# Early feed-forward work between expert matmuls: one piece for every second step, and the last pieces after the dynamic loop

## The chip, the core and the metric

The kernel runs on one NeuronCore of a Trainium2 chip. The metric is the device time of one execution, in microseconds (us). Three runs of the kernel before gave 2300.58, 2306.05 and 2307.99; the median is 2306.05. TensorE (PE) does the matmuls, ScalarE (ACT) and VectorE (DVE) the elementwise work and GpSimd (POOL) a little of it; SyncE (SP) issues the loads of the weights, in the order of its program.

## The reference, cut to what matters

The program computes two transformer blocks. The first ends in a mixture of 16 experts over 256 tokens, two experts for each token; the second begins with a half feed-forward layer on 256 latent tokens (the first block's output) and, with the same weights, on 256 context tokens (an input of their own):

```
# block 1, end: 16 experts, y added to h
for e in range(N_EXPERTS):
    hidden = jax.nn.silu(xt @ w_exp_gate[e]) * (xt @ w_exp_up[e])     # 1024 -> 512
    y = y + combine[:, e:e + 1] * (hidden @ w_exp_down[e])            # 512 -> 1024
# block 2, start: the same weights for latent (h_x) and context tokens (h_c)
h_x = _half_ffn(h_x, ..., ffn1_up[l], ffn1_down[l])
h_c = _half_ffn(h_c, ..., ffn1_up[l], ffn1_down[l])                   # D_FF = 2816
```

The context tokens don't depend on block 1. Their feed-forward work can therefore be done during the experts.

## The kernel before

**Early work.** The 2816 hidden channels are 22 tiles of 128, worked off in parts of 6, 6, 6 and 4 tiles. For the context tokens of the first layer the second part (6 tiles) is done early, by the generator `early_ffn` (L1036). It gives up control (`yield`) 32 times: 24 times in the up projection, each time after 12 matmuls of 256 columns (tile `pab`), and 8 times in the down projection, after 18 of them (`pd` from `eH`, `eL`). So there are 288 early up matmuls and 144 early down matmuls. The weights of a tile are first split in two by ACT (L225) and DVE or POOL (L228) into a tile `w`, of which there are two (`wspe`). `fill(n)` lets the generator run to its n-th next `yield`. Three calls with FILL = 3 stand ahead of the experts and use 9 of the 32.

**Experts.** `experts` (L1082) takes the 16 experts in 8 pairs (0 to 7). An expert works on up to 64 gathered tokens, so the two experts of a pair use one half of TensorE's columns each. In a pair:
- gate and up (tile `egu`, L1151): two halves of gate, two of up, called steps here; each step needs one chunk of 1 MB of each expert and has 8 rows in the built program (4 for each expert);
- silu on ACT (`es`, L1161), the product on DVE (L1162), a transpose on TensorE (`ept`, L1165), its copy on DVE (`hT`, L1168);
- down (tile `ey`, L1177): two steps with one chunk of each expert; the split of `y` by ACT and DVE; scatter to the tokens (`eo`, L1191 and L1192).

After pairs 0 and 2 stands the gather of the tokens of the next two pairs (`xgp`, 32 matmuls). `self.fill(1)` stands behind each of the six steps (L1155, L1180), so that 6 pieces are handed out in a pair, until there are no more.

**Loads.** `rawtile` gives a chunk one of seven 8 KB buffers, three in the pool `raw` and four in `rawm`, in a fixed alternation of the pools; two more tiles (`spare`) serve once. A buffer is free again when its last reader is done: a matmul for a chunk of an expert, the splits of both halves for a chunk of the early work. The early work's up weights are six chunks (three fetches of two), all fetched ahead of the experts; the third fetch lies in two of the four `rawm` buffers until it is split. The down weights are four chunks of 768 KB.

**The dynamic loop.** After pair 5 (LOOP_AT) a loop serves experts with more than 64 tokens (L1021 to L1027). In the profiled execution its body doesn't run. What stands behind it can't move ahead of it, and the seven chunks loaded ahead of it are the first of pair 6. The early work is used up there (L1017).

**What sets the order.** The program text gives priorities; a scheduler puts each engine's instructions in order by its own estimates when the program is built, and chooses the buffers. On the chip each engine follows its order.

Of the kernel before, what the change touches and what calls it, by code (L numbers as in the profile page):

```python
# [169 lines left out]
class Builder:  # L170
# [26 lines left out]
    def small(self, shape, name, dt=F32):  # L197
        return self.scr.tile(shape, dt, tag="sm_" + name, name=name, bufs=2)

    # ------------------------------------------------------------ weights  # L200
    def rawtile(self):
        if self.spare:
            return self.spare.pop(0)
# [72 lines left out]
                cons(c + i, p)  # L276
                yield True

    # ------------------------------------------------------------ norms
    def rsqrt(self, v, n, name):  # L280
        V = self.nc.vector
        y = self.small([128, n], name + "_y", I32)
# [99 lines left out]
        for _ in self.pending:  # L382
            pass

    # ------------------------------------------------------------ set-up
    def setup(self):
        nc, I = self.nc, self.I
        C = self.const
# [118 lines left out]
        o = self.voff[name] + j  # L507
        return self.vT[:, o:o + n]

    # ------------------------------------------------------------ modulation  # L510
    def ada(self, l, n, on_vector):
        V, mm = self.nc.vector, self.nc.tensor.matmul
        ps = self.mm("ada_ps")
# [58 lines left out]
        for l, n in lns:  # L572
            yield from self.ada(l, n, True)

    # ------------------------------------------------------------ feed-forward
    def ffn(self, l, n, up, dn, vs, side, pace, after):
        nc = self.nc
        self.raw_n, self.raws = 0, 7
# [105 lines left out]
        hs = self.h[:, d, v * S:(v + 1) * S]  # L684
        self.nc.vector.scalar_tensor_tensor(hs, p, self.gmod[:, l, n, d, v:v + 1], hs, ALU.mult, ALU.add)  # L685

    # ------------------------------------------------------------ block 1
    def to_tokens(self, src, dst, nt, ch0):
        nc = self.nc
        p = self.mm("tt")  # L690
        for t in range(nt):
            nc.tensor.transpose(p[:, t * 128:(t + 1) * 128], src[:, t * 128:(t + 1) * 128], self.ident)
        nc.scalar.activation(dst[:, 0:nt, ch0:ch0 + 128],
                             p[:, :128 * nt].rearrange("p (t c) -> p t c", c=128), AF.Copy)
# [267 lines left out]
        yield from self.proj(self.I["w_sb_out"][0], 0, 4, 0, 8, act, S,  # L962
                             lambda t, p: nc.vector.tensor_tensor(gates[:, t, :], p, gates[:, t, :], ALU.mult))

    # ------------------------------------------------------------ experts
    def moe(self):
        nc, I = self.nc, self.I
        V = nc.vector
        self.raw_n, self.raws = 0, 7
        with self.sub("hn", 1) as Q, self.sub("hide", PARTS[EARLY]) as E, self.sub("moe", 1) as P, \  # L970
                self.sub("wspe", 2) as self.wsp, self.sub("moew", 1) as W, self.sub("rawm", 4) as self.raw_more:
            hH = [Q.tile([128, 1024], F32R, name=f"hnH{t}") for t in range(2)]
            hL = [Q.tile([128, 1024], F32R, name=f"hnL{t}") for t in range(2)]
            rs = self.rs
            self.early = self.early_ffn(E)
            self.fill(FILL)
            comb, sel = self.route(self.lg, rs, P)
            self.fill(FILL)
            pp = self.mm("pos")
            nc.tensor.matmul(pp[:, 0:16], self.before, sel[:, 0, :], start=True, stop=True)  # L980
            nc.tensor.matmul(pp[:, 16:32], self.before, sel[:, 1, :], start=True, stop=False)
            nc.tensor.matmul(pp[:, 16:32], self.ones, sel[:, 0, :], start=False, stop=True)
            for t in range(2):
                nc.tensor.matmul(pp[:, 32:48], self.ones, sel[:, t, :], start=(t == 0), stop=(t == 1))
            mc = P.tile([128, 1], F32, name="mc")
            V.tensor_reduce(mc, pp[:, 32:48], AX.X, ALU.max)
            mi = P.tile([128, 1], I32, name="mi")
            V.tensor_scalar(mi, mc, -1.0, None, ALU.add)
            V.tensor_scalar(mi, mi, 6, None, ALU.logical_shift_right)
            pos = P.tile([128, 2, 16], F32, name="pos")  # L990
            V.scalar_tensor_tensor(pos, pp[:, :32].rearrange("p (t e) -> p t e", t=2), 1.0, sel,
                                   ALU.add, ALU.mult)
            V.tensor_scalar(pos, pos, -1.0, None, ALU.add)
            for t in range(2):
                for q in range(2):
                    p = self.a2("hnt")[:, 0, :] if q else self.mm("hnt")
                    for j in range(4):
                        nc.tensor.transpose(p[:, j * 128:(j + 1) * 128],
                                            self.h[:, q * 4 + j, t * 128:(t + 1) * 128], self.ident)
                    hi, lo = hH[t][:, q * 512:(q + 1) * 512], hL[t][:, q * 512:(q + 1) * 512]  # L1000
                    nc.scalar.activation(hi, p, AF.Copy, scale=rs[:, t:t + 1])
                    V.scalar_tensor_tensor(lo, p, rs[:, t:t + 1], hi.bitcast(F32), ALU.mult, ALU.subtract)
            self.fill(FILL)
            self.gates_of_route()
            order = [(p, c) for p in range(8) for c in range(12)]
            ready = {pc: self.expert_chunk(*pc) for pc in order[:AHEAD]}
            self.spare = [P.tile([128, 2048], F32, tag="xg", name="raw", bufs=2),
                          W.tile([128, 2048], F32, tag="y", name="raw")]
            ready.update({pc: self.expert_chunk(*pc) for pc in order[AHEAD:AHEAD + 2]})
            self.on_pool = 0  # L1010
            self.gs = P.tile([128, 8], F32, name="gs")
            pos2 = P.tile([128, 2, 16], F32, name="pos2")
            V.tensor_copy(pos2, pos)
            for p in self.experts(pos, comb, hH, hL, P, W, ready):
                if p != LOOP_AT:
                    continue
                for _ in self.early:  # L1017
                    pass
                ready.update({(p + 1, c): self.expert_chunk(p + 1, c) for c in range(7)})
                with self.tc.issue_after(self.loaded.ins):  # L1020
                    more = nc.values_load(mi[0:1, 0:1], min_val=0, max_val=3)  # L1021
                self.raw_loop = self.wsp
                with self.tc.If(more > 0):
                    with self.tc.For_i(0, more, 1):
                        V.tensor_scalar(pos2, pos2, -64.0, None, ALU.add)
                        for _ in self.experts(pos2, comb, hH, hL, P, W, {}):
                            pass  # L1027
                self.raw_loop = None
            self.raw_more = None
        self.pending = self.two_norms(self.sums)  # L1030

# [4 lines left out]
    def early_ffn(self, E):  # L1036
        nc, I = self.nc, self.I
        up, dn = I["ffn1_up_2"][0], I["ffn1_down_2"][0]
        f0, nf = sum(PARTS[:EARLY]), PARTS[EARLY]
        sl = slice(S, 2 * S)  # L1040
        hid = []

        def fetch(c):
            c0 = (f0 + 2 * c) * 128
            return [self.rows(up, 0, KD, m + c0, 256) for m in (0, NFF * 128)]

        nxt = fetch(0)
        for c in range(nf // 2):
            cur, nxt = nxt, fetch(c + 1) if 2 * c + 2 < nf else None
            for i in range(2):  # L1050
                p = self.mm("pab")
                for m in range(2):
                    w = self.split_w(cur[m][:, :, i * 128:(i + 1) * 128])
                    for ks in (range(4), range(4, KD)):
                        self.gemm(p[:, m * S:(m + 1) * S], w, self.xact(sl), ks=ks)
                        if m == 0 or ks[0] == 0:
                            yield True
                s, t = self.s512("fs")[:, :S], self.s512("ft")[:, :S]
                nc.scalar.activation(s, p[:, :S], AF.Silu)
                nc.vector.tensor_tensor(t, s, p[:, S:], ALU.mult)  # L1060
                hid.append([E.tile([128, S], F32R, tag=x, name=x) for x in ("eH", "eL")])
                self.split_a(*hid[-1], t)
                yield True
        for dc in range(4):
            v = self.rows(dn, f0 * 128, nf, dc * 256, 256)
            for i in range(2):
                w = self.split_w(v[:, :, i * 128:(i + 1) * 128])
                p = self.mm("pd")[:, :S]
                self.gemm(p, w, lambda f: hid[f])
                self.residual(p, 2 * dc + i, 0, 0, 1)  # L1070
                yield True

    def expert_chunk(self, p, c):
# [8 lines left out]
    def experts(self, pos, comb, hH, hL, P, W, ready):  # L1082
# [57 lines left out]
        for p in range(8):  # L1140
# [4 lines left out]
            for m in range(2):  # L1145
                for kh in range(2):
                    for aa in both:
                        w = {a: chunk(p, m * 4 + kh * 2 + a) for a in aa}
                        for kk in range(4):
                            for a in aa:  # L1150
                                mm(pr[a * 64:a * 64 + 64, m, :],  # L1151
                                   xg[p // 2][:, kh * 4 + kk, es[a] % 4 * 64:es[a] % 4 * 64 + 64], w[a][:, kk, :],
                                   start=(kh == 0 and kk == 0), stop=(kh == 1 and kk == 3))
                    if self.raw_loop is None:
                        self.fill(1)  # L1155
            if p % 2 == 0:
                slot_gates(p // 2)
# [12 lines left out]
            for fh in range(2):  # L1170
                for aa in both:
                    w = {a: chunk(p, 8 + fh * 2 + a) for a in aa}
                    for ff in range(2):
                        f = fh * 2 + ff
                        for n in range(2):
                            for a in aa:
                                mm(y[a * 64:a * 64 + 64, n, :], hT[:, f, a * 64:a * 64 + 64],  # L1177
                                   w[a][:, ff, n * 512:(n + 1) * 512], start=(f == 0), stop=(f == 3))
                if self.raw_loop is None:
                    self.fill(1)  # L1180
            y2 = W.tile([128, 2, 1024], F32R, tag="y", name="y")
            yH, yL = y2[:, 0, :], y2[:, 1, :]
# [123 lines left out]
        V.tensor_tensor(o1, o1, o2, ALU.add)  # L1306
        spread(comb, o1)

    # ------------------------------------------------------------ block 2 mixing
    def mix(self, l):  # L1310
        nc, I = self.nc, self.I
        full = l == 0
# [404 lines left out]
            nc.vector.tensor_scalar(z, p, self.vec("ps", l * 2 + j), None, ALU.mult)  # L1717
            self.split_a(self.xH[:, 2 + j, :NX], self.xL[:, 2 + j, :NX], z)

    # ------------------------------------------------------------ all of it  # L1720
    def finish(self):
        nc = self.nc
        r = self.rstd(self.sq)
# [59 lines left out]
```

## Time and profile before

| | us |
|---|---|
| time, three runs | 2300.58, 2306.05, 2307.99 |
| median | 2306.05 |
| profiled execution, span from first to last instruction | 2303.4 |
| experts, first gate matmul of pair 0 to the scatter of pair 7 | 313.7 to 619.2 |

The page gives the profiled execution's span and no other time of it; the span lies 2.7 below the median of the runs. A row of the trace's views names the source line, the engine, the operation and the tiles (out<-in). A matmul row of the built program is recorded as two instructions in `egu` and `ey`: a step's 8 rows are 16 instructions in the profile.

### The profile page before, as it was taken

How to read it: one execution, taken by the hardware profiler on the slowest of the kernel's cores; microseconds unless marked ns; L12 is line 12 of the kernel's file. 1: busy time of each engine (PE TensorE's matmuls, PEld its weight loads, DVE VectorE, ACT ScalarE, POOL GpSimd, SP SyncE). 2: the span in 40 equal slices, each digit the busy share in tenths (PEclk: the TensorE clock that was granted, in tenths of full speed). 3: DMA queues.
4: the chain of work that ended last, by engine and by line, in shares of the span. 5: the costliest groups of instructions: out<-in, count | busy, mean ns of one | idle time of the engine just before them, and what ended most of it. 6: DMA issues, size and time to landing. Idle time of an engine off the chain costs nothing.

```text
span 2303.4 us, 32441 instructions
## 1 busy us (share of the span) xinstructions
PE 2233.4 (97%) x13295; PEld 1818.9 (79%) x13295; DVE 1441.0 (63%) x2516; ACT 817.1 (35%) x1256; POOL 163.3 (7%) x160
## 2 busy tenths in 40 slices
PE   8999999997999999999999999999999999999998
PEld 8789974643488977877887777789777888879998
DVE  5656852221288778766678777637874335877676
ACT  4554431100132322346642222224222223475443
POOL 0200100000000000330220000001000002311000
PEclk9999999999899999999999999999999999999999
DMA  8673858897945645320135555424543222316551
GB/s 257 204 243 127 276 200 321 321 394 314 355 147 197 234 162 169 97 86 28 56 129 194 185 169 180 140 91 139 187 158 120 83 74 63 109 41 218 186 174 47
DMA packets 273174, 395.91 MB, mean 172 GB/s; under 512 B 18156, under 2 KB 220540, under 8 KB 260604
## 3 DMA queue, kind: packets, MB, share of 16 engines
q1 hardware_dynamic: 272000, 392.33, 49.7%
q8 instruction: 106, 1.74, 0.3%
q0 software_dynamic: 576, 1.18, 0.2%
q14 instruction: 48, 0.39, 0.1%
q10 hardware_dynamic: 444, 0.27, 0.0%
HBM read 392.71 MB, written 1.05 MB: 171 GB/s over the span
## 4 chain that ended last, share of the span: by engine, by line
PE 69%; DVE 4%; ACT 1%; POOL 1%; issue 1%; ACTq 0%; DVEq 0%; POOLq 0%
PE pab L241 12%; PE pab L242 12%; PE pab L243 12%; PE pd L241 6%; PE pd L242 6%; PE pd L243 6%; PE pj L242 2%; PE pj L243 2%; PE pj L241 2%; PE ada_ps L522 1%; PE egu L1151 1%; PE aT L1636 1%; DVE xL L330 1%; PE as L1607 1%; PE ao L1653 1%; PE po L241 1%
## 5 line engine op out<-in xcount | busy, mean ns | idle before, releaser
L225 ACT ACTIVATE w<-raw 128x1024 fp32r<-128x1024 f32 (+2 forms) x432 | 425.8, 990 | 703.5 <-PE pd L243 239.9
L228 DVE TENSOR_TENSOR w<-raw,w 128x1024 fp32r<-128x1024 f32 (+2 forms) x422 | 479.2, 1145 | 185.0 <-ACT w L225 183.0
L242 PE MATMUL pab<-xL,w 128*128 128x512 f32 (+2 forms) x1600 | 551.5, 345 | 2.3 <-DVE xL L330 1.1
L241 PE MATMUL pab<-xH,w 128*128 128x512 f32 (+2 forms) x1600 | 553.3, 346 | 0.2
L243 PE MATMUL pab<-xH,w 128*128 128x512 f32 (+2 forms) x1600 | 551.2, 345 | 1.4 <-POOL w L228 1.4
L241 PEld LDWEIGHTS pab<-xH,w 128*128 128x128 f32 x1600 | 302.8, 189 | 62.6 <-issue 20.0
L243 PEld LDWEIGHTS pab<-xH,w 128*128 128x128 f32 x1600 | 302.7, 189 | 44.5 <-issue 3.2
L242 PEld LDWEIGHTS pab<-xL,w 128*128 128x128 f32 x1600 | 302.4, 189 | 43.8 <-DVE xL L330 2.4
L539 DVE SCALAR_TENSOR_TENSOR acc<-raw,sT,acc 128x512 f32<-128x512 f32 x420 | 284.8, 744 | 0.0
L241 PE MATMUL pd<-hH,w 128*128 128x512 f32 (+1 forms) x800 | 267.2, 336 | 0.3 <-ACT hH L232 0.2
L242 PE MATMUL pd<-hL,w 128*128 128x512 f32 (+1 forms) x800 | 267.0, 335 | 0.0
L243 PE MATMUL pd<-hH,w 128*128 128x512 f32 (+1 forms) x800 | 266.4, 334 | 0.0
L241 PE MATMUL pj<-xH,w 128*128 128x256 f32 (+1 forms) x816 | 252.9, 311 | 9.3 <-ACT w L225 3.8
L242 PE MATMUL pj<-xL,w 128*128 128x256 f32 (+1 forms) x816 | 247.8, 304 | 7.2 <-DVE xL L330 6.5
L243 PE MATMUL pj<-xH,w 128*128 128x256 f32 (+1 forms) x816 | 247.0, 303 | 0.5 <-DVE w L228 0.5
L241 PEld LDWEIGHTS pj<-xH,w 128*128 128x128 f32 x816 | 158.3, 195 | 24.8 <-ACT w L225 5.1
L242 PEld LDWEIGHTS pj<-xL,w 128*128 128x128 f32 x816 | 159.0, 195 | 13.1 <-DVE xL L330 7.8
L241 PEld LDWEIGHTS pd<-hH,w 128*128 128x128 f32 x800 | 151.2, 190 | 21.2 <-issue 3.4
L685 DVE SCALAR_TENSOR_TENSOR h<-pd,gmod,h 128x256 f32<-128x256 f32 x224 | 100.8, 478 | 104.5 <-PE pd L243 104.2
L243 PEld LDWEIGHTS pd<-hH,w 128*128 128x128 f32 x800 | 151.4, 190 | 16.8 <-issue 1.7
L242 PEld LDWEIGHTS pd<-hL,w 128*128 128x128 f32 x800 | 151.8, 190 | 15.4 <-DVE hL L233 0.2
L243 PEld LDWEIGHTS pj<-xH,w 128*128 128x128 f32 x816 | 158.9, 195 | 5.7 <-DVE w L228 0.8
(388 smaller groups left out, 2508.8 us busy)
## 6 DMA issues: line engine op xcount, KB each, us to landing
raw<-ffn_up SPq DMA_DIRECT2D x94, 1024.0 KB, 5.3
raw<-w_ada SPq DMA_DIRECT2D x72, 1024.0 KB, 5.0
raw<-ffn_down SPq DMA_DIRECT2D x52, 768.0 KB, 4.8
raw<-w_in SPq DMA_DIRECT2D x32, 1024.0 KB, 5.4
raw<-w_exp_gate SPq DMA_DIRECT2D x32, 1024.0 KB, 8.2
raw<-w_exp_up SPq DMA_DIRECT2D x32, 1024.0 KB, 7.9
raw<-w_exp_down SPq DMA_DIRECT2D x32, 1024.0 KB, 7.3
raw<-w_gate SPq DMA_DIRECT2D x8, 1024.0 KB, 5.8
```

Of the source, the lines that this page charges most:

```text
L225: self.nc.scalar.activation(wh, v, AF.Copy)
L228: e.tensor_tensor(wl, v, wh.bitcast(F32), ALU.subtract)
L241: mm(o, wH[:, k, :], aH, start=(first and k == 0), stop=False)
L242: mm(o, wH[:, k, :], aL, start=False, stop=False)
L243: mm(o, wL[:, k, :], aH, start=False, stop=(last and k == n - 1))
L330: nc.vector.scalar_tensor_tensor(lo, t, B(j), hi.bitcast(F32), ALU.add, ALU.subtract)
L522: mm(ps[g * 32:(g + 1) * 32, :], self.unit[:, 31 - r:63 - r], acc[v], start=(u < 2), stop=(u > 3))
L539: ins = V.scalar_tensor_tensor(acc[v], w[:, g, :], s, acc[v], ALU.mult, ALU.add)
L685: self.nc.vector.scalar_tensor_tensor(hs, p, self.gmod[:, l, n, d, v:v + 1], hs, ALU.mult, ALU.add)
L1151: mm(pr[a * 64:a * 64 + 64, m, :], xg[p // 2][:, kh * 4 + kk, es[a] % 4 * 64:es[a] % 4 * 64 + 64], w[a][:, kk, :], start=(kh == 0 and kk = ...
L1607: mm(o[:, c], qs, x[i][:, c], start=(i == 0 and not (near and c.start == 0)), stop=(i == 1))
L1636: nc.tensor.transpose(T[:, j * 128:(j + 1) * 128], e[:, a, j * 128:(j + 1) * 128], self.ident)
```

## The change

The change calls `fill(1)` after every second step only (the second half of gate, of up and of down), so that a pair gets 3 pieces. Ahead of the dynamic loop, the early work is no longer used up: it only goes on to the end of a down chunk (`early_open`), and a last loop behind the experts takes what would be left. By the count of the calls, pairs 0 to 5 get 18 pieces, one more closes a chunk, and the last 4 (two down chunks) go to pairs 6 and 7.

```diff
@@ moe
             for p in self.experts(pos, comb, hH, hL, P, W, ready):
                 if p != LOOP_AT:
                     continue
-                for _ in self.early:
-                    pass
+                while self.early_open:
+                    self.fill(1)
                 ready.update({(p + 1, c): self.expert_chunk(p + 1, c) for c in range(7)})
...
                 self.raw_loop = None
+            for _ in self.early:
+                pass
             self.raw_more = None
@@ early_ffn
         nxt = fetch(0)
+        self.early_open = True
...
                 self.residual(p, 2 * dc + i, 0, 0, 1)
+                self.early_open = i == 0
                 yield True
@@ experts
-                    if self.raw_loop is None:
+                    if self.raw_loop is None and kh:
                         self.fill(1)
...
-                if self.raw_loop is None:
+                if self.raw_loop is None and fh:
                     self.fill(1)
```

The rest of the diff only empties comment lines. In the built program lines behind the change stand 2 to 4 further down (L1151 becomes L1155). On TensorE the rows from the first gate matmul of pair 0 to the end of the experts change place; before and behind them the order of kinds is the same.

TensorE at the end of pair 0, before (`xgp` is the gather, `ept` the transpose of the silu's product):

```order
L1110 MATMUL xgp<-xH,hnL_3109 128x256
L1165 MATMUL ept<-sqc,es 128x128 x4
L241 MATMUL pab<-xH,w 128x256
L242 MATMUL pab<-xL,w 128x256
L243 MATMUL pab<-xH,w 128x256
```

The same place now:

```order
L1155 MATMUL egu<-raw,xg 64x512 x7
L1169 MATMUL ept<-sqc,es 128x128 x4
L1181 MATMUL ey<-raw,hT 64x512
L1155 MATMUL egu<-raw,xg 64x512
L1181 MATMUL ey<-raw,hT 64x512 x15
L1195 MATMUL eo<-xL,y 128x256 x2
L1155 MATMUL egu<-raw,xg 64x512 x2
```

Before, 23 gather matmuls stood between the last gate and up row and the transposes, and 8 early ones behind these; now the transposes follow the last gate and up row at once, and the down rows follow the transposes.

SP's queue, loads of pair 1, before. Numbers name the tiles; in brackets is what a load waits for (PE or DVE: the reader of the buffer's last content; DMAHW: an earlier transfer):

```order
L214 DMA raw_3720<-w_exp_gate 128x2048 [waits DMAHW2_49,PE_49]
L214 DMA raw_3772<-w_exp_up 128x2048 [waits DMAHW1_49]
L214 DMA raw_3746<-w_exp_up 128x2048 [waits DVE_49]
L214 DMA raw_3808<-w_exp_down 128x2048 [waits DMAHW3_49,PE_49]
L214 DMA raw_3810<-w_exp_down 128x2048 [waits DMAHW6_49,PE_49]
L214 DMA raw_3840<-w_exp_down 128x2048 [waits DVE_49]
L214 DMA raw_3842<-w_exp_down 128x2048 [waits DMAHW4_49,DMAHW0_49,PE_49]
```

Loads of pair 1 now:

```order
L214 DMA raw_3657<-w_exp_gate 128x2048 [waits DMAHW5_49,DMAHW2_49,PE_49]
L214 DMA raw_3695<-w_exp_up 128x2048 [waits DMAHW6_49]
L214 DMA raw_3697<-w_exp_up 128x2048
L214 DMA raw_3683<-w_exp_up 128x2048 [waits DMAHW3_49,PE_49]
L214 DMA raw_3730<-w_exp_down 128x2048 [waits DMAHW5_49,PE_49]
```

And some of pair 2 now:

```order
L214 DMA raw_3959<-w_exp_down 128x2048 [waits DMAHW5_49,PE_49]
L214 DMA raw_3845<-w_exp_up 128x2048 [waits DMAHW2_49,PE_49]
L214 DMA raw_3855<-w_exp_up 128x2048 [waits DVE_49]
L214 DMA raw_3969<-w_exp_down 128x2048 [waits DVE_49]
L214 DMA raw_3971<-w_exp_down 128x2048 [waits DMAHW3_49,DMAHW0_49,PE_49]
```

The two loads that take the buffers of the third up fetch (those that wait for DVE) were pair 1's `raw_3746` and `raw_3840`; now they are pair 2's `raw_3855` and `raw_3969`.

SP's queue behind the dynamic loop, before:

```order
L214 DMA raw_5937<-w_exp_up 128x2048 [waits DMAHW1_49,DMAHW0_49,PE_49]
L214 DMA raw_5974<-w_exp_down 128x2048 [waits DMAHW2_49,DMAHW1_49,PE_49]
L214 DMA raw_5976<-w_exp_down 128x2048 [waits DMAHW3_49,DMAHW2_49,PE_49]
L214 DMA raw_5986<-w_exp_down 128x2048 [waits DMAHW4_49,DMAHW3_49,PE_49]
L214 DMA raw_5988<-w_exp_down 128x2048 [waits DMAHW5_49,DMAHW4_49,PE_49]
```

And now:

```order
L214 DMA raw_5833<-ffn1_down_2 128x6x256 [waits DMAHW7_49,DMAHW6_49,PE_49]
L214 DMA raw_5866<-w_exp_up 128x2048 [waits DMAHW7_49,DMAHW0_49,PE_49]
L214 DMA raw_5926<-w_exp_down 128x2048 [waits DMAHW1_49,DMAHW0_49,PE_49]
L214 DMA raw_5928<-w_exp_down 128x2048 [waits DMAHW2_49,DMAHW1_49,PE_49]
L214 DMA raw_5938<-w_exp_down 128x2048 [waits DMAHW3_49,DMAHW2_49,PE_49]
```

A chunk of the early down weights now goes first, ahead of pair 6's last up chunk.

## Rows read from the trace of the kernel before

**Rows 1.** First line of the page, and its busiest engine.

```profile
span 2303.4 us, 32441 instructions
PE 2233.4 (97%) x13295; PEld 1818.9 (79%) x13295; DVE 1441.0 (63%) x2516; ACT 817.1 (35%) x1256; POOL 163.3 (7%) x160
```

**Rows 2.** Stretches: length, busy PE, PEld, DVE, ACT, POOL, granted clock, DMA share, GB/s.

```profile
313.70:503.00 189.30, 184.57 (x982) 100.73 (x983) 49.53 (x79) 29.14 (x47) 0.00 (x0) 1.00 0.84 326
503.00:620.00 117.00, 98.70 (x453) 43.06 (x449) 23.07 (x38) 12.03 (x20) 0.00 (x0) 0.93 0.85 344
```

**Rows 3.** Who waited for whom, PE, 480 to 620: sum, times, longest us.

```profile
PE xgp L1107 <- DVE xH L1096: 6.5, 1, 6.5
PE ept L1165 <- DVE es L1162: 5.2, 4, 1.5
PE eo L1192 <- DVE y L233: 4.3, 9, 0.9
PE ey L1177 <- DVE hT L1168: 3.1, 4, 0.8
PE eo L1191 <- ACT y L232: 1.4, 2, 0.7
```

**Rows 4.** The same view of PE from 300 to 480.

```profile
PE ept L1165 <- DVE es L1162: 1.5, 1, 1.5
PE egu L1151 <- DMA raw<-w_exp_up: 0.6, 1, 0.6
```

**Rows 5.** PE in order of time, late pairs: start, length, in brackets idle before.

```profile
489.11 10.51 PE L1151 MATMUL egu<-raw,xg 128*64 128x512 f32 x46
...
550.71 0.57 PE L1107 MATMUL xgp<-xH,hnH 128*128 128x256 f32 x1 [6.49 <-DVE xH L1096]
...
558.42 13.95 PE L1151 MATMUL egu<-raw,xg 128*64 128x512 f32 x64
...
574.43 0.74 PE L1165 MATMUL ept<-sqc,es 128*128 128x128 f32 x4 [0.76 <-DVE es L1162]
...
589.02 13.95 PE L1151 MATMUL egu<-raw,xg 128*64 128x512 f32 x62
```

**Rows 6.** PE in order of time: the first step of pair 0, then pair 2.

```profile
313.71 3.65 PE L1151 MATMUL egu<-raw,xg 128*64 128x512 f32 x16
...
403.40 3.65 PE L1151 MATMUL egu<-raw,xg 128*64 128x512 f32 x16
406.99 0.38 PE L241 MATMUL pab<-xH,w 128*128 128x256 f32 x1
...
408.61 1.07 PE L1151 MATMUL egu<-raw,xg 128*64 128x512 f32 x2
409.61 0.38 PE L241 MATMUL pab<-xH,w 128*128 128x256 f32 x1
...
411.24 7.08 PE L1151 MATMUL egu<-raw,xg 128*64 128x512 f32 x30
418.25 0.38 PE L241 MATMUL pd<-eH,w 128*128 128x256 f32 x1
```

**Rows 7.** Loads into `raw` issued from 350 to 356: issue to landing.

```profile
DMA to landing us min/median/max: 4.8/6.4/8.0
```

**Rows 8.** SP's own waits before issuing loads, 310 to 545.

```profile
SPq L214 <- DVE w L228: 17.1, 5, 7.3
```

**Rows 9.** The down matmuls of pairs 4, 5, 7 alone: columns as in rows 2, without POOL.

```profile
502.00:510.00 8.00, 7.09 (x32) 2.21 (x32) 0.00 (x0) 0.22 (x1) 1.00 1.00 418
531.00:541.00 10.00, 8.78 (x32) 2.61 (x32) 0.50 (x1) 0.60 (x1) 0.83 1.00 415
605.00:615.00 10.00, 8.78 (x32) 2.60 (x32) 0.00 (x0) 0.20 (x1) 0.83 1.02 344
```

**Rows 10.** Costliest groups: the split of the weights; busy us, mean ns, idle before.

```profile
L225 ACT ACTIVATE w<-raw 128x1024 fp32r<-128x1024 f32 (+2 forms) x432 | 425.8, 990 | 703.5 <-PE pd L243 239.9
L228 DVE TENSOR_TENSOR w<-raw,w 128x1024 fp32r<-128x1024 f32 (+2 forms) x422 | 479.2, 1145 | 185.0 <-ACT w L225 183.0
```

## The prediction

> **What bounds the kernel now.** The page's first lines: TensorE is busy 97% of a span of 2303.4 us [rows 1]. That is the whole program; the change touches the experts, so the next view is the stretches [rows 2]. From 313.7 to 503 (pairs 0 to 4, gate and up) TensorE is busy 184.6 of 189.3 us while the DMA engines are at 0.84; from 503 to 620 it is busy only 98.7 of 117, with a granted clock of 0.93. The waits then say for what. After 480 TensorE waits 6.5 us for the first gather behind the dynamic loop, 5.2 in four waits for the silu's product, 3.1 in four for the copy `hT`, 5.7 for `y`, and never for a load [rows 3]. Before 480 there is one wait of 1.5 for the silu and one of 0.6 for a load [rows 4]: there the early matmuls and gathers lie in the gaps. So early pairs are full of matmuls, late pairs have gaps of 1.5 + 0.8 (silu, transposes' copy) and some 1 to 1.7 (`y`), which nobody fills. No engine but TensorE ends the stretch, and behind it the order of kinds is the same in both kernels: what pair 7 is late, the end is late.
>
> **Prices.** Eight `egu` rows (a step) take 406.99 − 403.40 = 3.59, one row 1.00, 15 rows 7.01 [rows 6]: two rows run side by side on the two column halves in a slot of 0.86, a single row takes a slot too, and a run costs 0.14 more. Twelve early matmuls take 408.61 − 406.99 = 1.62 [rows 6], fitted by 0.118 each and 0.2 for a run. Thirty-two gathers take 558.42 − 550.71 = 7.7 [rows 5], 0.24 each; the matmuls for the slots' gates 1.3 (574.43 − 0.76 − 572.37) [rows 5]. A load lands 4.8 after its issue at the least [rows 7], and loads in line follow each other by 2.5 (1.049 MB at 418 GB/s) [rows 9]. A split of a weight half takes 0.99 + 1.15 [rows 10].
>
> **What is moved.** No matmul is added or removed: 323 early ones (179 up, 144 down) stand among the experts in both orders, and their 38 us stay on TensorE. By the order, 240 of 288 up matmuls are done when pair 2's gate and up end, against 288 and 18 down before, and all 144 down ones come behind pair 4's gate and up, 72 of them behind the loop. The slots of `egu` and `ey` fall from 205 to 203 (fewer single rows), runs of experts' rows from 39 to 35, early runs rise from 26 to 27: −1.7 − 0.6 + 0.2 = **−2.1**.
>
> **Waits for silu and copy.** The pieces that covered them go. In the new order the transposes follow the last gate and up row at once in pairs 0 to 5, and the down rows follow the transposes in all but pair 3. That makes five times 1.5 + 0.8, 1.5 in pair 3, and 0.8 in pair 6, whose silu wait lies behind 18 early matmuls and the slots' gates: 13.8. Before, up to pair 7's last up row, it was 1.5 in pair 1 [rows 4], then 2.3, 2.3 and 1.5 [rows 3]: 7.6. **+6.2**. Waits for `y` get 0.8 shorter: pairs 5 and 6 now have early matmuls there, pairs 0 and 1 have lost theirs. **−0.8**.
>
> **Waits for loads.** The early work also holds buffers. The third up fetch sits in two of the seven until it is split, and that needs 216 and 240 early up matmuls done. Before, pair 1's loads took these buffers over; now pair 2's do. Pairs 0 to 2 so run on five buffers, and a load can only go out when a matmul just ahead has freed one. SP's waits for a split exist already, 17.1 us in five [rows 8], and cost TensorE nothing while seven buffers run ahead. Now I follow the new order with the prices above. Pair 0: from 313.7, 9 rows (4.4), 23 early (2.9), slots' gates 1.3, 24 gathers (5.7), 9 early (1.3) and 16 rows (7.0) end at 336.3. There the buffer of the first up chunk comes free, the last up chunk goes out as the third in line, and lands at about 342; TensorE has 3 early matmuls and 8 gathers left and is through at 338.8. Wait: 3.2. The remaining steps give 1.1 for pair 0's down, 0.7 for pair 1's gate, 3.4 for pair 1's up (its buffer is freed at 373.1, it lands at 378.1, TensorE is ready at 374.7), 3.2 for pair 1's second down step, and 1.0 for pair 2's up (split ready at 424.6, load there 4.9 later). Behind the loop a down chunk of the early work goes out only when pair 6's first step has freed a buffer, and its split ends 2.1 after TensorE wants it. Sum 14.7, against 0.6 before [rows 4]: **+14.1**. From pair 3 to 5 seven buffers run ahead and I find no wait. The trace shows no run with five buffers, so both ends: 0 if the loads still come in time, and +27 if the four waits of 3 grow by the 3.2 between the shortest and the longest landing [rows 7]. I take 14, from the shortest.
>
> The page "DMA: Bandwidth & Descriptors" of the Trainium skill (Bandwidth, Measured) gives 6.15 us for 1 MB, for loads issued from GpSimd. The trace has 4.8 from issue to landing on SP's queue [rows 7], and it decides; by the page's price the four long waits would add 5 and the time would be 2329.
>
> **The clock.** Pair 5's and pair 7's down matmuls take 8.78 instead of pair 4's 7.09, at a granted clock of 0.83 instead of 1.00 [rows 9]: part of them ran at 1.2 GHz, behind the silu and copy waits. Such a drop costs 1.7, and it came in three of the four late pairs, in two ahead of pair 7's last up row. The new order has six such places ahead of it and four load waits of 2 to 3 us. I count the two that were there, as before, and leave the others to the range: 1.7 each.
>
> **Sum.** −2.1 + 6.2 − 0.8 + 14.1 = +17.4. As a check, following the whole order puts the end of pair 4's gate and up at 495.5, against 489.11 + 10.51 = 499.6 before [rows 5]: 4 us won with 144 down matmuls (17 us and their runs) not yet done. It puts pair 7's last up row at 614.3 with no clock drop, 617.7 with two, against 589.02 + 13.95 = 603.0 [rows 5]: +14.7. The two ways differ by 2.7; I take the sum. The profiled execution becomes 2303.4 + 17.4 = 2320.8 in span. The runs' median lies 2.7 above that span: 2306.05 + 17.4 = 2323.5, **2324**.
>
> **Rivals.**
> - *The gaps are filled (faster).* Late pairs have 117 − 98.7 = 18.3 idle, 11.8 without the loop's 6.5 [rows 2, 3]. If the 144 moved matmuls sat in them while pairs 0 to 3 get shorter by their 17, the experts would win 11.8: 2294. For it: DMA is used at 0.84 early, TensorE is not full late [rows 2]. It decides from the point where pair 3 ends earlier by more than the late pairs get longer, that is, if pair 4's gate and up ended ahead of some 485. Against: by the order only pair 6's silu and some `y` waits have early matmuls beside them; the others lie inside gate and up, where nothing waits. Chance 0.07.
> - *Loads come in time (no change).* Without the load waits the sum is +17.4 − 14.1 = +3.3: 2309. For: the loads' longest landing, 8.0, is one in a full line [rows 7]. Against: the chunk that pair 0's last step needs is not even issued before the step ahead of it is done. Chance 0.12.
> - *The clock falls more often (slower still).* Four more drops and load waits longer by 3.2 each: 17.4 + 6.8 + 12.8 = +37, 2343. For: three of four such gaps lowered it. Against: a drop ahead of a load wait is absorbed by it. Chance 0.09.
>
> The page "Perfetto Trace Analysis" of the Trainium skill (Optimization Strategy) says that regimes with different bottlenecks may gain from being interleaved. That is the first rival's mechanism, and the stretches do show two regimes; by that rule the time is 2294, and it would be right if moved matmuls met the gaps.
>
> **How the numbers follow.** My forecast has 0.72 (2314 to 2334), the rivals 0.07, 0.12 and 0.09. A difference under 0.3% (7 us) can't be told from none here. Faster is the first rival: 0.07. Within 0.3% is the second and a small tail of mine: 0.13. Slower: 0.80. The range runs from 2308, about the second rival, to 2338, short of the third's end.
>
> **What would show it.** Right: PE waits for DMA on `raw` of pairs 0 to 2 (gate, up and down), together 10 to 18 us; silu waits in five more or less equal pieces from pair 0 on; pair 4's gate and up ending 2 to 6 us earlier than before, pair 7's 13 to 20 later; SP waiting for the split longer than 17 us. Wrong: no DMA wait on TensorE up to 440, or pair 4 ending ahead of 485; or all of this, and the time made good behind the experts.

## The result, and the profile after

The changed kernel took 2320.61 us (median of 4 runs, 2316.18 to 2324.18) where the kernel before took 2307.02 beside it: a ratio of 1.0074, with a 95% interval of 1.0058 to 1.0091. A second comparison on another chip, six runs of the changed kernel beside twelve of before, gave 1.0093 (1.0075 to 1.0110). The ratios here are not quotients of the two medians: 2320.61 to 2307.02 alone would be 1.0059. It is slower, by 0.7 to 0.9%, some 17 to 21 us by the ratios; the medians lie 13.6 us apart in the first comparison and 21.9 in the second. 17.4 was forecast.

The page's first lines of the profiled execution after, against [rows 1]:

```profile
span 2322.4 us, 32441 instructions
PE 2233.8 (96%) x13295; PEld 1814.9 (78%) x13295; DVE 1440.6 (62%) x2516; ACT 816.8 (35%) x1256; POOL 162.9 (7%) x160
```

The span is 19.0 us longer with as many instructions. Where the time went is read from one view of each kernel, TensorE alone, from the first gate row of pair 0 to pair 7's last gate and up row. The columns are the stretch, its length, busy PE (instructions), granted clock, DMA share and GB/s. Before:

```profile
313.70:603.00 289.30, 270.56 (x1376) 0.98 0.85 337
```

After:

```profile
313.94:624.90 310.96, 275.34 (x1376) 0.96 0.81 316
```

The same 1376 instructions take 21.7 us more. Idle time is length less busy time: 18.7 before, 35.6 after, so 16.9 of it are waits and 4.8 are matmuls that run longer. The waits of TensorE after, from 300 to 480 (sum, times, longest), where [rows 4] had two lines:

```profile
PE egu L1155 <- DMA raw<-w_exp_up: 6.5, 3, 3.0
PE ept L1169 <- DVE es L1166: 6.1, 4, 1.6
PE ey L1181 <- DMA raw<-w_exp_down: 3.3, 2, 1.9
PE ey L1181 <- DVE hT L1172: 2.4, 3, 0.8
PE eo L1195 <- ACT y L232: 1.4, 2, 0.7
PE egu L1155 <- DMA raw<-w_exp_gate: 0.6, 1, 0.6
PE xgp L1111 <- ACT xg L1118: 0.5, 1, 0.5
PE eo L1196 <- DVE y L233: 0.2, 1, 0.2
PE pab L241 <- DVE h L1198: 0.2, 1, 0.2
```

Loads are waited for six times, 10.4 us in all. From 480 to 650, against [rows 3]:

```profile
PE xgp L1111 <- DVE xH L1100: 6.2, 1, 6.2
PE ept L1169 <- DVE es L1166: 5.2, 4, 1.5
PE ey L1181 <- DVE hT L1172: 3.1, 4, 0.8
PE eo L1196 <- DVE y L233: 2.1, 4, 0.9
PE eo L1195 <- ACT y L232: 1.0, 2, 0.7
PE pd L241 <- ACT w L225: 0.8, 1, 0.8
```

The late pairs have their four silu and four copy waits as before, although 72 early matmuls now stand behind the loop: only the waits for `y` fell. The places are seen in TensorE's timeline (start, length, in brackets the idle time before), answering to [rows 5, 6]:

```profile
342.10 3.27 PE L1155 MATMUL egu<-raw,xg 128*64 128x512 f32 x8 [2.33 <-DMA raw<-w_exp_up]
...
379.30 5.16 PE L1155 MATMUL egu<-raw,xg 128*64 128x512 f32 x16 [2.98 <-DMA raw<-w_exp_up]
...
443.40 8.78 PE L1181 MATMUL ey<-raw,hT 128*64 128x512 f32 x32 [0.78 <-DVE hT L1172]
...
494.14 10.51 PE L1155 MATMUL egu<-raw,xg 128*64 128x512 f32 x46
...
617.79 7.09 PE L1155 MATMUL egu<-raw,xg 128*64 128x512 f32 x32
```

Pair 0 and pair 1 wait for an up chunk. Right behind these waits 16 `egu` instructions take 5.16 us where [rows 6] has 3.65, and pair 2's down matmuls take 8.78. The granted clock there (columns as above):

```profile
341.00:345.00 4.00, 2.90 (x8) 0.57 0.72 238
378.90:382.50 3.60, 3.20 (x8) 0.53 0.44 182
402.50:406.50 4.00, 3.28 (x10) 0.57 0.97 410
443.40:452.20 8.80, 8.80 (x33) 0.81 0.84 321
542.10:551.00 8.90, 8.83 (x33) 0.81 0.83 316
```

In the first three TensorE ran most of the time at 1.2 GHz, in the last two for part of it. Before, the granted clock was 1.00 up to 503 [rows 2].

### The profile page after: what moved, and what is told of

It is laid out like the page before. It is cut to its first block, busy times and chain, and to the rows that moved or that the text cites. A ratio compares the mean times of both kernels' runs of the same rounds, so it can differ in the third digit from the quotient of the medians.

```text
span 2322.4 us, 32441 instructions
## 1 busy us (share of the span) xinstructions
PE 2233.8 (96%) x13295; PEld 1814.9 (78%) x13295; DVE 1440.6 (62%) x2516; ACT 816.8 (35%) x1256; POOL 162.9 (7%) x160
## 4 chain that ended last, share of the span: by engine, by line
PE 68%; DVE 4%; ACT 1%; issue 1%; POOL 1%; DMA 0%; ACTq 0%; DVEq 0%; POOLq 0%
PE pab L241 12%; PE pab L242 12%; PE pab L243 12%; PE pd L241 6%; PE pd L242 6%; PE pd L243 6%; PE pj L242 2%; PE pj L241 1%; PE pj L243 1%; PE ada_ps L522 1%; PE aT L1640 1%; PE egu L1155 1%; PE as L1611 1%; PE ao L1657 1%; DVE xL L330 1%
```

## The experiments

All ratios are to runs of the kernel before on the same chip, with 95% intervals. Three dots mark what is left out of an edit; comments behind `#` in the edits stand here for the reader.

**Which half of the change costs.** Half pace alone: the early work is used up ahead of the loop again.

```diff
-                while self.early_open:
-                    self.fill(1)
+                for _ in self.early:
+                    pass
```

> The half pace alone: fill after every second step as in the changed kernel, but the early work is used up ahead of the dynamic loop as before. Pairs 0 to 5 then have the order of the changed kernel, and 90 down matmuls stand in front of the loop. My theory (the cost is made in pairs 0 to 2: load waits of some 10 us, silu and copy waits of some 8, clock drops behind them): the time stays at the changed kernel's, 2318 to 2325 us; pair 6's silu wait of 1.5 us comes back and the wait for a split behind the loop (0.8) goes. Rival (the part behind the loop costs): back to 2307.

Measured: 2324.64 us, 1.0093 (1.0079 to 1.0108). Load waits of pairs 0 to 2 are 9.4 us, the silu waits of pairs 0 to 3 6.1, those of pairs 4 to 7 5.2, as in the changed kernel: pair 6's did not come back, since it had not gone. The part behind the loop alone (the changed kernel with the full pace of before in pairs 0 to 5, stopped after 28 pieces until the loop is passed; the down steps get the same condition):

```diff
     def fill(self, n):
         for _ in range(n):
+            if self.fills == 28 and not self.looped:
+                return
+            self.fills += 1
...
-                    if self.raw_loop is None:
+                    if self.raw_loop is None and (kh or p < 6):
...
```

> The part behind the loop alone: full pace as before in pairs 0 to 3, but it stops after 28 of the 32 pieces, and the last 4 (72 down matmuls, 8.5 us) go to pairs 6 and 7. My theory: pairs 0 to 2 are as before, with no load wait over 1 us; pair 3 loses the cover of its silu and copy waits (+2.3) and pair 6 gains one (-1.5) and a shorter y wait (-0.8): 2303 to 2310 us, no difference from before. Rival (the part behind the loop costs): 2315 to 2322.

Measured: 2304.40 us, 1.0002 (0.9991 to 1.0013). And the changed kernel again, beside runs of before on one more chip:

> The changed kernel once more, beside the same runs of the kernel before, so that the half pace alone (1.0093) and the version with unread matmuls in the silu gaps (1.0074) can be set against it with more runs. My theory: 1.006 to 1.009 of before; the half pace alone is then the whole change, within 0.3%. Rival (the part behind the loop wins back a third of it): under 1.006.

Measured: 2324.43 us, 1.0093. So the half pace alone is as slow as the whole change, and the part behind the loop is worth nothing either way: its trace has 2.3 us more of silu and copy waits up to 480 (pair 3 lost its cover) and 1.2 us less for `y` behind. Pair 6's silu wait stays at 0.75 (0.76 in [rows 5]), though 18 early matmuls stand ahead of it, for the product also waits for the slots' gates, which come behind them.

**Load waits and held buffers.** The third up fetch issued late, so that it doesn't lie in two buffers through pairs 0 and 1:

```diff
-            cur, nxt = nxt, fetch(c + 1) if 2 * c + 2 < nf else None
+            cur, nxt = nxt, fetch(c + 1) if c == 0 else None
             for i in range(2):
+                if c == 1 and i == 1:
+                    nxt = fetch(2)
```

> The changed kernel, but the third up fetch of the early work (two chunks of 1 MB) is issued only midway through the second, so that it doesn't hold two buffers through pairs 0 and 1. My theory (held buffers make the load waits): of the 10.4 us of load waits in pairs 0 to 2 fewer than 4 are left, the silu waits of 1.5 stay in pairs 0 to 3, and the time is 2307 to 2313 us. Rival (loads come late for want of bandwidth, or the load waits hide time that is lost otherwise): load waits move to other places and the time stays at 2318 to 2324.

Measured: 2309.10 us, 1.0031 (1.0019 to 1.0042). Its waits for loads from 300 to 480:

```profile
PE ey L1183 <- DMA raw<-w_exp_down: 2.5, 2, 1.4
PE egu L1157 <- DMA raw<-w_exp_up: 2.0, 2, 1.2
```

4.5 us are left of 10.4, a little more than the "fewer than 4" that was expected, and more than half of the loss is gone, with three silu waits still there. Not all of it is loads: TensorE's order moved with the edit, so that one silu and one copy wait (2.3 us) are gone up to 480 as well. Now the other way: the loads untouched, the silu covered.

```diff
-                    if self.raw_loop is None and kh:
+                    if self.raw_loop is None and kh and not m:
                         self.fill(1)
...
+            if self.raw_loop is None:
+                with self.tc.issue_after(last.ins):   # last: the last gate and up matmul
+                    self.fill(1)
             pt = self.mm("ept")
```

> The changed kernel, but the piece behind a pair's up step is set between the last gate and up row and the transposes, so that 12 or more early matmuls cover the silu in pairs 0 to 6. The buffers are held as long as in the changed kernel or a little longer. My theory (silu waits and the clock drops behind them are one half of the cost, load waits the other): no silu wait is left up to pair 6 (6.1 us in pairs 0 to 3 and 3.7 behind go), fewer drops of the clock, load waits of 8 to 15 us stay: 2309 to 2316 us. Rival (only the uncovered gaps cost, the load waits don't): 2304 to 2308. Rival (only the load waits cost): 2318 to 2324.

Measured: 2333.71 us, 1.0142 (1.0124 to 1.0160), against all three expectations. No silu wait is left up to pair 6, but its load waits from 300 to 480 are:

```profile
PE egu L1155 <- DMA raw<-w_exp_up: 12.6, 4, 4.1
PE egu L1155 <- DMA raw<-w_exp_gate: 7.6, 3, 3.3
PE ey L1184 <- DMA raw<-w_exp_down: 5.8, 2, 4.4
```

That is 26.0. By its order only 192 early up matmuls are done when pair 2's gate and up end, 240 in the changed kernel; the third fetch, which needs 216 and 240, lies in its buffers longer. So load and silu waits don't simply add, as my theory had it: covering the silu with work that comes later costs more in held buffers than it wins. Both edits together:

> Both single edits together: the changed kernel with the third up fetch issued late (two buffers free in pairs 0 and 1) and with a piece between gate and up and the transposes. With the piece alone, load waits rose to 26 us and the time to 2334; with the late fetch alone they fell to 4.5 us and the time to 2309. My theory (held buffers make the load waits, so covering the silu pays only where no buffer is held for it): load waits of 4 to 10 us, no silu wait up to pair 6, 2302 to 2310 us. Rival (the pieces between gate and up and the transposes themselves delay the loads' release): load waits stay above 20 us and the time above 2322.

Measured: 2309.01 us, 1.0023 (1.0008 to 1.0038), with 12.1 us of load waits. It stands where the late fetch alone does: of the silu and copy waits that the cover saves (12.2 down to 1.6 us up to pair 7's last up row), load waits take back 7.6 and waits for `y` 1.8. The 12.1 lie between the two expectations (4 to 10, and above 20). So the late fetch takes away 14 of the 26.0 us; whether the rest comes from the pieces' new places, or from a hold that the late fetch only shortens, no run separates. And fewer buffers at the full pace:

```diff
-        self.raw_n, self.raws = 0, 7
+        self.raw_n, self.raws = 0, 6
...
-                self.sub("wspe", 2) as self.wsp, self.sub("moew", 1) as W, self.sub("rawm", 4) as self.raw_more:
+                self.sub("wspe", 2) as self.wsp, self.sub("moew", 1) as W, self.sub("rawm", 3) as self.raw_more:
...
-                ready.update({(p + 1, c): self.expert_chunk(p + 1, c) for c in range(7)})
+                ready.update({(p + 1, c): self.expert_chunk(p + 1, c) for c in range(6)})
```

> The kernel before, at its full pace, with six buffers for the chunks instead of seven (and six chunks instead of seven loaded ahead of the loop). My theory (two held buffers of seven are what the half pace costs): one buffer fewer costs load waits of 4 to 12 us in pairs 0 to 2 while the third fetch holds two of the six, little behind: 2309 to 2318 us. Rival (the load waits of the changed kernel come from when its matmuls stand, not from the number of buffers): under 2 us of load waits, 2302 to 2307.

Measured: 2320.07 us, 1.0086 (1.0060 to 1.0112), a little above the expected 2309 to 2318: with one buffer of seven less the kernel loses as much as by the whole change. Load waits are 11.5 before 480, and 3.6 behind. The scheduler also placed the early matmuls of pair 0 otherwise, so not all of it is the buffer alone. The kernels side by side; the middle columns are for the same 136.2 us of each trace, in which the slower kernels get less far:

| kernel | load waits 300 to 480 | PE busy 313.8 to 450 | DMA share there | ratio |
|---|---|---|---|---|
| before | 0.6 | 134.08 | 0.79 | 1 |
| third fetch late | 4.5 | 126.01 | 0.79 | 1.0031 |
| both edits | 12.1 | 122.50 | 0.75 | 1.0023 |
| six buffers, full pace | 11.5 | 119.28 | 0.69 | 1.0086 |
| changed kernel | 10.4 | 116.49 | 0.69 | 1.0074, 1.0093 |
| silu covered | 26.0 | 111.56 | 0.63 | 1.0142 |

Load waits alone don't order the ratios: both edits have more of them than the changed kernel, but 1.6 us of silu and copy waits up to pair 7's last up row where that has 14.5. In the kernels with long load waits the DMA engines work less, not more. Nor does a load take longer on its way: the five of the changed kernel that are issued from 320 to 345 land, against [rows 7],

```profile
DMA to landing us min/median/max: 4.8/5.6/6.6
```

after their issue. Loads come late because they are issued late, not for want of bandwidth. The page "Perfetto Trace Analysis" of the Trainium skill (Optimization Strategy) says that a gap which repeats on the engine that should be saturated can mean too few buffers for the next tile. These runs agree, with the DMA share falling from 0.79 to 0.63 beside it.

**The clock by itself.** Eleven matmuls that nobody reads, in the silu gaps, so that TensorE works there and nothing else changes place:

```diff
+            if self.raw_loop is None and p != 6:          # before: p > 3
+                with self.tc.issue_after(last.ins):
+                    x = self.mm("dum")
+                    for _ in range(11):
+                        last = mm(x[:, :256], hH[0][:, :128], hL[0][:, :256], start=True, stop=True)
             pt = self.mm("ept")
```

> The changed kernel with 11 further matmuls of 256 columns, whose result nobody reads, between the last gate and up row and the transposes of every pair but 6: TensorE works through the silu's 1.5 us instead of waiting, and neither the order of the rest nor any load's buffer changes. My theory (the clock drops cost time of their own, on top of the waits): the drops behind silu and copy waits (in pairs 2, 5 and 7) go, those behind load waits (pairs 0 and 1) stay, and the time falls by about 1.7 us for each drop less, 3 to 7 us: 2312 to 2318 us where the changed kernel has 2318 to 2324. Rival (the drops follow something else, or time won is lost behind the experts): the time stays within 2 us of the changed kernel's.

Measured: 2318.26 us, 1.0074 (1.0057 to 1.0091), at the upper end of the expected 2312 to 2318. In the trace the drops behind the silu gaps of pairs 2, 5 and 7 are gone; TensorE in those three stretches, which hold a few other matmuls too (the 32 down ones alone take 7.09 in each):

```profile
443.00:452.00 9.00, 8.22 (x38) 1.00 0.99 393
538.00:549.00 11.00, 10.12 (x51) 1.00 0.97 360
626.00:636.00 10.00, 8.51 (x41) 1.00 0.96 317
```

Those behind load waits stay, and pair 6's down matmuls, without one in the changed kernel (7.09), now take 8.78. Its load waits up to 480 are 11.7 us for 10.4, and up to pair 7's last up row the trace takes 312.7 us, within the 310.9 and 313.9 of the changed kernel's two traces. Against 1.0093 on one chip and 1.0074 on the other the gain can't be told from none: inconclusive. Nor does a drop stand in the same pair each time: with the half pace alone pair 2's down matmuls took 7.09 and pair 4's 8.76, in an order that is the changed kernel's up to there. In the kernel before, whose late pairs have no load waits:

> The kernel before with the same 11 unread matmuls in the silu gaps of pairs 4 to 7, where it has no early work. My theory (as for the changed kernel): the three drops behind the down rows of pairs 5, 6 and 7 go, 1.7 us each, and the half-clock stretch behind the experts gets shorter or stays: 2296 to 2302 us where the kernel before has 2304 to 2307. Rival (the drops cost nothing that the end shows): 2303 to 2307.

Measured: 2297.60 us, 0.9986 (0.9974 to 0.9998). The stretches of the down matmuls of pairs 4 to 7, against [rows 9]; they hold 1 to 10 other matmuls each, and the 32 down ones alone take 7.09 in all four:

```profile
502.00:510.00 8.00, 7.65 (x34) 1.00 1.01 423
531.00:541.00 10.00, 8.80 (x42) 1.00 1.01 421
574.00:582.00 8.00, 7.54 (x34) 1.00 1.01 418
602.00:610.50 8.50, 7.20 (x33) 1.00 1.06 367
```

All four run at a granted clock of 1.00, with the copy waits of 0.8 still ahead of them. 0.14% is 3 us, of the 5 that three drops of 1.7 would give; the interval just excludes none. The profiled execution doesn't show the gain at its end: pair 7's last up row ends at 599.9, 3.1 us earlier than before, but the span is 2303.5. So the gain rests on the runs' times alone.

**Work put where the gaps are.** Up pieces at the full pace of before, so that buffers come free as before; the eight down pieces only in pairs 3 to 7, tied behind the last gate and up row (12 matmuls), behind the transposes (6), and in pairs 5 to 7 behind the down rows (18). For this the generator also gives up control twice inside a down piece, behind the split and behind 12 of the 18 matmuls:

```diff
+                    if self.raw_loop is None and p < 3 and self.ups:   # 15 up pieces
+                        self.ups -= 1
+                        self.fill(1)
+                    if self.raw_loop is None and p > 2 and m == kh == 0:
+                        self.fill(1)                                   # load and split
...
+            if self.raw_loop is None and p > 2:
+                self.fill_after(last)            # issue_after(last), then fill(1)
             pt = self.mm("ept")
...
+            if self.raw_loop is None and p > 2:
+                self.fill_after(last)
             y = self.a2("ey")
...
+                if self.raw_loop is None and p > 4:
+                    for _ in range(fh + 1):
+                        self.fill_after(last) if fh else self.fill(1)
```

> The 24 early up pieces at the full pace of before (used up in pair 2), and the 8 down pieces put into the gaps of pairs 3 to 7, tied there in TensorE's order: 12 early matmuls between the last gate and up row and the transposes, 6 between the transposes and the down rows, and in pairs 5 to 7 one piece of 18 between the down rows and the scatter. My theory (TensorE ends the stretch, and each gap that is covered without holding buffers is won): the silu and copy waits of pairs 3 to 7, 8.3 us in the trace of before, and 3 to 4 us of waits for y go, fewer clock drops follow them; against that stands the silu wait in pair 3 or 2 if a split is late, and part of the win may be given back behind the experts where the clock drops anyway: 2290 to 2298 us, 0.2 to 0.6% faster than before. Rival (the gaps don't set the end, as waits for loads or splits take their place): 2301 to 2308.

Measured: 2289.47 us (6 runs, 2288.34 to 2293.68), 0.9945 (0.9924 to 0.9967): faster than both kernels, and a little below the expected 2290 to 2298. Its waits from 480 to 650, all but the last line of 0.2:

```profile
PE xgp L1118 <- DVE xH L1107: 8.0, 1, 8.0
PE egu L1162 <- DMA raw<-w_exp_up: 5.4, 4, 1.4
PE eo L1214 <- DVE y L233: 0.9, 2, 0.7
PE egu L1162 <- DMA raw<-w_exp_gate: 0.3, 1, 0.3
```

No silu or copy wait stands there any more. New are load waits of 5.7 us, 5.4 of them in pairs 5 and 7 (four of 1.3 to 1.4): these pairs now run into the loads, at a DMA share of 1.02 and 1.06 in their down rows. What was won is read from the first gate row to the last scatter row (columns as above), before and in this kernel:

```profile
313.70:619.30 305.60, 282.79 (x1428) 0.97 0.85 334
312.26:609.30 297.04, 276.99 (x1428) 0.98 0.87 343
```

The same instructions take 8.6 us less (the whole span 11.5). Idle time falls only from 22.8 to 20.1, since load waits and a longer wait behind the loop (8.0 for 6.5) take the place of the covered gaps; the other 5.8 us are matmuls that run shorter. In pairs 4 to 7 the down matmuls now take 7.09 to 7.29, where three of the four took 8.64 to 8.78 before: about 5 of the 5.8. With the three `y` pieces put at the end of pair 2 instead:

> The kernel with the filled gaps, but the three pieces of 18 matmuls that stood between down rows and scatter in pairs 5 to 7 stand at the end of pair 2 instead; the silu and copy gaps of pairs 3 to 7 stay covered. That leaves one early down chunk instead of two to be loaded and worked off behind the loop. My theory (in the late pairs loads now end the wait, so a covered gap for y is partly paid back in load waits): the load waits behind 480 us, 5.7 us there, fall to 1 to 3 us, 3 to 4 us of waits for y come back, and the time is within 4 us of that kernel, 2287 to 2295. Rival (covered y gaps are won in full): 2294 to 2300.

Measured: 2290.95 us, 0.9959 (0.9940 to 0.9977), with 4.2 us of load waits behind 480 and 5.5 for `y`. The two can't be told apart: of the covered `y` gaps some 4.6 us were won and 1.5 paid back in loads, and what is left is under what the runs resolve. Load waits fell less than expected (1 to 3 us).

## Why the prediction was right, term by term

It forecast 2324 against 2321 and 2324 measured, by the mechanism that it names. The sum hides errors of both signs: loads were put 3.5 too high and the matmuls' own time 6.9 too low, and that these nearly cancel, with a few us given back behind the experts, is luck. (The 2.7 us between span and median are none of one execution's: each run's time lies 1.8 above its own span.) To pair 7's last up row:

| term | forecast | measured |
|---|---|---|
| slots and runs | −2.1 | with the clock, +4.8 |
| clock | 0 | (in the line above) |
| silu and copy waits | +6.2 | 14.5 − 7.5 = +7.0 |
| waits for `y` | −0.8 | 2.9 − 3.9 = −1.0 |
| waits for loads and the split | +14.1 | 11.2 − 0.6 = +10.6 |
| loop and others | 0 | −0.3 + 0.7 = +0.4 |
| sum | +17.4 | +21.8 (rounded rows; 21.7 as a whole) |

The measured waits are the rows above without pair 7's own (1.5 and 0.8 for silu and copy; for `y` 1.8 in both), which come later. The row's 0.7 more for silu is pair 6's, which I had taken to be covered. The trace of the second comparison gives +24.6 here: load and split waits 11.5 for 11.2, the matmuls 7.3 longer than before instead of 4.8.

*Waits for loads: right in kind, 3.5 too large.* Pair 0's up waited 2.3 where 3.2 was forecast, pair 1's 3.0 for 3.4, pair 1's second down step 1.9 and 1.4 together for 3.2; the split behind the loop 0.8 for 2.1. SP's queue after, from 310 to 545 (what it waited for before issuing a load), against [rows 8]:

```profile
SPq L214 <- DVE w L228: 17.5, 3, 9.6
```

17.5 against 17.1 passes the sign that the prediction set (longer than 17) but tells nothing; the longest, 9.6 for 7.3, tells more. That held buffers make most of these waits is shown by the late fetch (10.4 to 4.5, and 26.0 to 12.1 with the silu covered).

*The clock: the step that was mis-sized.* I counted two drops, as before, and took it that a drop ahead of a load wait is absorbed. Five stretches at 1.2 GHz stand ahead of pair 7's last up row, three of them right behind load waits, where the rows that ran late are on the path. By their rows they cost some 7.7 us together, the two of before 3.2; of the +4.8 in the table this leaves about +0.3 for slots and runs, where −2.1 was forecast. The check by walking the order shows it best: it put the end of pair 4's gate and up at 495.5, and it came at 504.7. To there the row is:

```profile
313.94:504.70 190.76, 169.48 (x832) 0.96 0.77 300
```

Idle are 21.3 us; the walk had 12.6 for loads and 8.4 for silu and copy, 21.0. That the sums agree to 0.3 is luck too: silu and copy measured 8.5, loads 10.4, and 2.3 are waits for `y` and others, for which the walk had nothing. The matmuls took 8.7 longer than the walk's prices: the four drops, at 1.3 to 1.7 each, are some 6 of that, and the rest is left to prices that were too low. The forecast signs on pair 4 (2 to 6 us earlier) and pair 7 (13 to 20 later; it was 21.9) therefore failed, while the time held.

*Behind the experts* I had said that what pair 7 is late, the end is late. Of 21.9 us 2.9 came back in the first trace: the granted clock of the 57 us behind pair 7's last up row was 0.91, where it was 0.85 before. In the trace of the second comparison, of the same kernel, it was 0.85 and next to nothing came back (21.6 later there, 21.4 at the end), so this belongs to the execution and not to the change.

*The rivals.* "Loads come in time" fell by the load waits. "The clock falls more often" was half right, in its drops and not in longer load waits. "The gaps are filled" fell for this change, but its mechanism is real in part: the last experiments put the down pieces into the gaps and won 0.55%, in the trace more by the faster matmuls behind the gaps than by the waits. What decided is what a piece holds and where it stands, not in which pair: in the changed kernel 144 down matmuls moved late and shortened no silu or copy gap of the late pairs, and four pieces moved late at the full pace, without the placing, gave 1.0002. The Trainium skill's page "Perfetto Trace Analysis" (Optimization Strategy) says that interleaving regimes with different bottlenecks may help; the 0.9945 agrees, and 1.0074 for the same idea, with held buffers and without the placing, shows the limit of it.

## What to carry to other kernels

Before you slow down work that is handed out between other work, ask what it holds while it waits: here two of seven buffers, and the loads of the main work paid. Move what holds little (the down pieces), keep what holds buffers at its pace, and tie a piece to the gap itself: left to the scheduler, the 144 down matmuls here covered no silu or copy gap. Count a wait with the slower matmuls behind it.

## What the runs showed of the hardware that was not expected

- A wait of 1.5 us with one of 0.8 behind it was followed by a stretch at 1.2 GHz in three of the six such places of the changed kernel (pairs 2, 5 and 7 of 0, 1, 2, 4, 5 and 7: down matmuls in 8.78 us instead of 7.09). With the 1.5 worked through and the 0.8 left, the down matmuls of the four late pairs of the kernel before all ran at 1.00.
- A wait of 2 to 3 us for a load, or of 1.9 and 1.4 with two instructions between, was followed by such a stretch in pairs 0 and 1, at a granted clock of 0.53 to 0.57: 16 `egu` instructions in 5.16 us instead of 3.65. Beside a wait of 2.98 us that is another 1.5. Four single load waits of 1.3 to 1.4 us in the kernel with filled gaps were not followed by one: the steps behind them took 3.65.
- The slow stretch behind the experts isn't fixed: the granted clock of the 57 us behind pair 7's last up row was 0.91 in one trace of the changed kernel and 0.85 in the other.
